# Two blocks of a network on one core: the order of the first loads, the first expert pair, the scattered pairs, and the start of the second block

## The chip, the cores and the metric

The kernel runs on one core of a Trainium2 chip. Its time is the device time of one execution in microseconds (us). Three runs of the kernel before gave 2696.38 us in the median, 2688.37 to 2698.73. All stages follow each other on that one core: TensorE (PE) with its weight loads (PEld), VectorE (DVE), ScalarE (ACT), GpSimd (POOL) and SyncE (SP), which mainly issues DMA transfers.

## The reference, cut to what matters

There are 512 tokens of 1024 channels in fp32 and a context of 256 rows. A first block is followed by a second one of two layers.

```python
# first block
m  = silu(c) @ w_mod + b_mod;  mc = silu(c_ctx) @ w_mod + b_mod      # shifts, scales, gates
hn = rmsnorm(x, g_norm1)*(1+sc1) + sh1;  cn = rmsnorm(ctx, g_norm1)*(1+csc1) + csh1
z  = hn @ w_in;  zc = cn @ w_in[:, OFF_BK:]     # the last 32 columns of w_in are the decay gates
h  = x + g1 * (concat(spatial_gating(z), gated_linear_attention(z, zc)) @ w_out)
hn2 = rmsnorm(h, g_norm2)*(1+sc2) + sh2
# router: 8 groups x 8 experts, top group, top 2 experts in it
for each chosen (token, expert):  y[token] += gate * (silu(t @ w1[e]) * (t @ w3[e])) @ w2[e]
h  = rmsnorm(h + g2*y, g_final)                 # input of the second block
# second block, layer 0: bidirectional DeltaNet and pooling mixer; layer 1: short convolution;
# each layer then a feed-forward in which each of 16 experts chooses its tokens; rmsnorm at the end
```

The 64 experts of the first block hold 3 x 64 matrices of 1024 x 512, some 403 MB.

## The kernel before

Six stages run one after the other; their rough places in the profiled execution are: mixer of the first block (mix1, 0 to 350 us), its 64 experts (moe1, 350 to 1489), mixer of layer 0 (mix2, to 1857), feed-forward (ec0, to 2165), mixer of layer 1 (mix3, to 2381), feed-forward and final norm (ec1, to the end). Each stage is a set of Python generators (tasks) which a planner, `weave`, interleaves by ranks and assumed times; a task yields an event, a count of free buffers, or a number of nanoseconds. The outcome is one fixed instruction sequence per engine. That sequence isn't always the order of the text: a POOL memset of `ch` (L2326), which the text puts late in the routing, runs at 5.77 us, and the cast of `wbg` (L448) stands on ACT ahead of the squares of `h`, which come earlier in the text. Engines run their sequence in order.

**Loads.** `pump` puts weight tiles (512 KB, or 256 KB) on SP's queue whenever the planner has a buffer for them; other transfers are issued by SP, POOL or ACT where the text has them. In `start` of mix1 SP issues `h` (x, 2 MB), `cx` (context, 1 MB), `wbg` (32 columns of w_in: 1024 pieces of 128 bytes), `w2g`, and then the 16 tiles of w_mod. POOL issues constants, and L635 writes zeros (`am`, repeated) into `yd`, a DRAM buffer of 4 MB into which the experts' outputs are later scattered. `cx` and `h` are squared on ACT, `rsqrt` makes 1/rms on DVE, `dg` is that on a diagonal, and 32 and 64 fp32 matmuls of `cx` and `h` against `dg` norm and transpose at once (`pT`). Then come the rows of the modulation (`pmr`, `pmt`, in `mod_rows`), which make A and B (L669, L670); the mixer's matmuls need these.

**Experts (`moe1`, `experts1`).** Two experts are one pair, 32 pairs in all, each with 24 weight tiles; 26 tile buffers stand ready when the stage begins, and a buffer is loaded again when PE has used it. `rank` gives each (token, expert) a slot (64 to an expert). For a pair, DVE makes the one-hot matrix P (L1252), PE takes token numbers out of it (`pid`), an indirect DMA on POOL gathers those rows of `xd` (the normed tokens, written to DRAM) into `xg` (L1240), eight transposes (`pxt`) and a scale and shift (`AB`, from `scales`) give `xT`, and PE computes `pab` (w1, w3), `phT` and `py` (w2). The first FAR = 28 pairs scatter their outputs to `yd` (L1351); after the last of them, `far` reads `yd` back in four tiles (`yg`, one buffer) and adds them to `h` (L1535). The last four pairs add theirs through matmuls against P (`pcm`, L1387), with their outputs split in two parts (`out_parts`, yh and yl). `ctx2` (the context's part of block 2) and `book` are woven among the pairs. `mods2` makes modulation rows of block 2 beside the end of mix1.

**Start of mix2.** `gfb` (g_final on all partitions) is loaded by POOL; u = h * gfb on DVE; ACT squares h and u; for each of four token tiles a chain of small DVE steps (`newton`) gives a norm `cf`, its diagonal goes to PE (`pT`); four more chains give `rf`. DVE also has the sums `macc` for the modulation of layer 0 (L2190), which wait for ada_w tiles.

## Time and profile before

| | us |
|---|---|
| three runs: median (lowest to highest) | 2696.38 (2688.37 to 2698.73) |
| the profiled execution's own time | 2696.17 |
| its span in the trace | 2694.4 |
| PE busy in it | 2362.1 (88%) |
| DVE busy | 1139.8 (42%) |
| ACT busy | 655.1 (24%) |
| POOL busy | 258.5 (10%) |
| DMA | 772.58 MB, mean 287 GB/s |

The mean granted TensorE clock was 0.951 of full speed. The page of the profile divides the span into 40 slices of about 67 us; in each it gives the busy share of each engine and of the 16 DMA engines in tenths. A busy share close to 1.0 in the DMA line means that the transfers set the pace there. The other views used are windows (busy time of each engine and the DMA share in a stretch), the timeline (instructions in order of time, with the idle time before each and what released it), and the waits (who was waited for, in total, how often, and the longest).

### The profile page before, as it was taken

Reading aid. Unit: us, or ns where it says so; the run is one execution under the profiler, and the core shown is the slowest. Engines: PE = TensorE matmul, PEld = TensorE weight load, DVE = VectorE, ACT = ScalarE, POOL = GpSimd, SP = SyncE. Lnnn points to the kernel's source line nnn. Section 1 sums busy time; section 2 is a strip of 40 time slices with the busy share of each in tenths; the row PEclk is TensorE's granted clock in tenths of the full one; section 3 lists DMA queues with packets and bytes.
Section 4 is the critical chain, followed back from the end, with each engine's and each line's share of the span. In section 5 each row is a group of like instructions: output and inputs, shape, how many; then the busy total and the mean of one; then the engine's idle time right before and its main releaser. Section 6 shows DMA issues by size and latency. Waiting matters only on the chain. (4 is left out here: it accounts for less than half of the span.)

```text
span 2694.4 us, 32948 instructions
## 1 busy us (share of the span) xinstructions
PE 2362.1 (88%) x11811; PEld 1302.3 (48%) x11811; DVE 1139.8 (42%) x2995; ACT 655.1 (24%) x1360; POOL 258.5 (10%) x257
## 2 busy tenths in 40 slices
PE   4899988899889988888869588897999989979997
PEld 3578743344333323332223467686544368854442
DVE  2878553322511111110122789696132287452223
ACT  3632432322102100111000444342211032331111
POOL 0000011001210000000000312322000010110000
PEclk9999988999999999999989799997999999989999
DMA  7545588999999999999996435535899776149984
GB/s 284 162 147 155 168 312 298 345 356 401 392 394 356 371 409 408 405 403 403 407 383 256 137 110 157 150 130 223 333 383 346 300 260 202 58 182 397 394 321 172
DMA packets 270337, 772.58 MB, mean 287 GB/s; under 512 B 42987, under 2 KB 54395, under 8 KB 269660
## 3 DMA queue, kind: packets, MB, share of 16 engines
q1 hardware_dynamic: 255964, 744.79, 74.0%
q0 software_dynamic: 12768, 23.15, 2.5%
q10 hardware_dynamic: 1440, 2.52, 0.3%
q8 instruction: 94, 1.54, 0.2%
q14 instruction: 71, 0.58, 0.1%
HBM read 767.11 MB, written 26.74 MB: 295 GB/s over the span
## 5 line engine op out<-in xcount | busy, mean ns | idle before, releaser
L1403 PE MATMUL pab<-w,xT 128*64 128x512 f32 x3072 | 814.9, 603 | 18.8 <-DMA w<-in_w_dram 18.6
L1403 PEld LDWEIGHTS pab<-w,xT 128*64 128x64 f32 x3072 | 237.4, 137 | 470.8 <-issue 353.1
L1403 PE MATMUL py<-w,hT 128*64 128x512 f32 x1536 | 378.1, 631 | 35.6 <-ACT hT L1335 32.2
L1403 PEld LDWEIGHTS py<-w,hT 128*64 128x64 f32 x1536 | 116.1, 142 | 224.8 <-issue 164.5
L386 ACT CAST wh<-w 128x512 fp32r<-128x512 f32 (+2 forms) x160 | 110.1, 695 | 227.9 <-PE pg L466 185.6
L387 DVE TENSOR_TENSOR wl<-w,wh 128x512 fp32r<-128x512 f32 (+2 forms) x160 | 134.5, 849 | 63.7 <-ACT wh L386 57.5
L1327 DVE TENSOR_TENSOR hh<-hh,pab 128x512 f32<-128x512 f32 x32 | 22.0, 687 | 328.1 <-PE pab L1403 328.0
L1387 DVE TENSOR_TENSOR h<-h,pcm 128x512 f32<-128x512 f32 x160 | 102.4, 682 | 100.4 <-PE pcm L466 100.3
L1299 ACT ACTIVATE xT<-pxt,AB 128x128 f32<-128x128 f32 x190 | 70.0, 464 | 243.0 <-PE pab L1403 224.6
L466 PE MATMUL pg<-xh,wh 128*128 128x512 f32 x288 | 118.8, 416 | 9.6 <-DVE cv L1675 9.5
L1345 DVE TENSOR_TENSOR yf<-py,g 128x512 f32<-128x512 f32 x56 | 36.2, 686 | 210.6 <-PE py L1403 210.6
L466 PE MATMUL pg<-xl,wh 128*128 128x512 f32 x288 | 115.6, 401 | 0.0
L466 PE MATMUL pg<-xh,wl 128*128 128x512 f32 x288 | 115.5, 402 | 0.0
L1325 ACT ACTIVATE hh<-pab 128x512 f32<-128x512 f32 x32 | 19.1, 597 | 371.0 <-PE pab L1403 371.0
L2190 DVE SCALAR_TENSOR_TENSOR macc<-w,c,macc 128x512 f32<-128x512 f32 x116 | 89.7, 776 | 28.7 <-DMA w<-in_ada_w_dram 15.3
L1176 DVE TENSOR_TENSOR hh<-hh,pab 128x512 f32<-128x512 f32 x16 | 11.0, 687 | 188.5 <-PE pab L1403 188.5
L472 PE MATMUL phT<-CA,hh 128*128 128x128 f32 x192 | 32.6, 294 | 63.2 <-DVE hh L1327 52.7
L1240 POOL DMA_INDIRECT xg<-xd,nt x32 | 33.0, 1030 | 525.1 <-PE pxt L472 510.3
L466 PE MATMUL pcm<-yh,PT 128*128 128x512 f32 x160 | 67.8, 437 | 9.7 <-ACT yh L1378 9.5
L1377 DVE SCALAR_TENSOR_TENSOR yo<-py,gt,g 128x512 f32<-128x512 f32 x40 | 30.0, 751 | 105.5 <-PE py L1403 103.8
L1378 ACT CAST yh<-yo 128x512 fp32r<-128x512 f32 x40 | 24.7, 618 | 203.4 <-DVE yo L1377 203.4
L466 PE MATMUL pdis<-P,xh 128*128 128x256 f32 x256 | 68.1, 303 | 4.6 <-DVE P L1107 4.6
(758 smaller groups left out, 3777.7 us busy)
## 6 DMA issues: line engine op xcount, KB each, us to landing
w<-in_w_dram SPq DMA_DIRECT2D x768, 512.0 KB, 10.2
w<-in_w_gate_dram SPq DMA_DIRECT2D x128, 512.0 KB, 9.1
w<-in_w_up_dram SPq DMA_DIRECT2D x128, 512.0 KB, 10.1
w<-in_w_down_dram SPq DMA_DIRECT2D x128, 512.0 KB, 8.2
w<-in_ada_w_dram SPq DMA_DIRECT2D x164, 256.0 KB, 3.1
w<-in_w_mod_dram SPq DMA_DIRECT2D x64, 256.0 KB, 2.9
w<-in_sc_w_in_dram SPq DMA_DIRECT2D x24, 512.0 KB, 5.3
w<-in_w_in_dram SPq DMA_DIRECT2D x40, 256.0 KB, 2.8
```

The lines of the kernel that those rows point to most:

```text
L386: nc.scalar.copy(hi, raw)
L387: nc.vector.tensor_tensor(lo, raw, hi.bitcast(F32), op=ALU.subtract)
L466: ins = self.nc.tensor.matmul(out, lhsT, rhs, start=start, stop=stop)
L472: self.nc.tensor.transpose(out, in_, self.ident if ident is None else ident)
L1240: nc.gpsimd.indirect_dma_start(out=xg[pr % len(xg)], out_offset=None, in_=xd, in_offset=bass.IndirectOffsetOnAxis(ap=d, axis=0), bounds_ch ...
L1299: nc.scalar.activation(xT[:, k0 + k, :], p[:, k * 128:(k + 1) * 128], AF.Identity, scale=self.Af[:, k0 + k:k0 + k + 1], bias=self.Bf[:, k0 ...
L1345: nc.vector.tensor_tensor(y[:, c * 512:(c + 1) * 512], ps[c], self.g2[:, c * 512:(c + 1) * 512], op=ALU.mult)
L1377: nc.vector.scalar_tensor_tensor(y, p[:rows], gate[:rows], self.g2[:rows, c * 512:(c + 1) * 512], op0=ALU.mult, op1=ALU.mult)
L1378: nc.scalar.copy(yh[:rows], y)
L1387: self.nc.vector.tensor_tensor(self.h[:, i, cs], self.h[:, i, cs], p, op=ALU.add)
L1403: self.nc.tensor.matmul(out, lhsT, rhs, start=start, stop=stop)
L2190: nc.vector.scalar_tensor_tensor(acc, w, s, acc, op0=ALU.mult, op1=ALU.add)
```

## The change

- First loads: `cx` is issued before `h`; `wbg` is issued after `pump`, behind all the weight tiles that `pump` has queued on SP by then; `w2g` goes to POOL's queue, ahead of POOL's constants.
- The zeros for `yd` stand at the end of `start` in the text, behind the splits of the modulation.
- `scales` (the pfc matmuls and the copy to AB) moves from the start of `moe1` into the routing tail of mix1; the later rows of `mods2` are held until the rank is made.
- First expert pair: no token numbers and no gather. Pr = P * r (four DVE steps) and 32 fp32 matmuls of h against Pr give the scaled, transposed tokens directly. The three gather buffers are for later pairs.
- FAR goes from 28 to 30, so two pairs are left to `pcm`; yh and yl have two buffers instead of three in this stage; the work tiles of the pairs are allocated up front.
- mix2: the row of g_final is loaded when moe1 begins; the eight `newton` chains become two vector `rsqrt`, one for cf and one for rf.

```diff
-FAR = 28
+FAR = 30
@@ first loads, mix1
+        cx = bg.tile([128, NTC, D], F32, tag="cx", name="cx")
+        nc.sync.dma_start(cx, a["ctx"].rearrange("(i p) d -> p i d", p=128))
         if self.h_in is None:
             nc.sync.dma_start(self.h, a["x"].rearrange("(i p) d -> p i d", p=128))
-        cx = bg.tile([128, NTC, D], F32, tag="cx", name="cx")
-        nc.sync.dma_start(cx, a["ctx"].rearrange("(i p) d -> p i d", p=128))
-        wg = self.t512(tp, "wbg")[:, 0:KD * 32].rearrange("p (k f) -> p k f", k=KD)
-        nc.sync.dma_start(wg, w_in[:, BG:BG + 32].rearrange("(k p) f -> p k f", p=128))
-        w2 = cp.tile([33, 512], F32, name="w2g")
-        nc.sync.dma_start(w2, a["w_gate2"])
...
         self.pump()
+        wg = self.t512(tp, "wbg")[:, 0:KD * 32].rearrange("p (k f) -> p k f", k=KD)
+        nc.sync.dma_start(wg, w_in[:, BG:BG + 32].rearrange("(k p) f -> p k f", p=128))
+        w2 = cp.tile([33, 512], F32, name="w2g")
+        nc.gpsimd.dma_start(w2, a["w_gate2"])
@@ consts() loses, start() gets at its end
+            nc.gpsimd.dma_start(self.yd.rearrange("(p r) d -> p r d", p=128),
+                                am.rearrange("p a b c t -> p (a b c t)").unsqueeze(1).to_broadcast([128, 2 * T // 128, D]))
@@ tail, after the rank; mod_rows
             self.rk = self.rank(self.Mb, NE1)
+            self.fire(evr, 0)
...
         for j in range(len(wants)):
+            if j and hold:
+                yield hold
@@ experts1: feed, and the transposes of pair 0
                 if not pr:
-                    yield rG
-                    yield 700
-                    fetch(pr, number(Pq, tok, 2 * pr, T, "nt"))
+                    Pr = work.tile([128, NT, 128], F32, tag="PT", name="Pr", bufs=3)
+                    for i in range(NT):
+                        nc.vector.tensor_scalar(Pr[:, i, :], Pq(i).bitcast(F32), self.r[:, i:i + 1], None, op0=ALU.mult)
+                    hot.append(Pr)
+                    self.fire(evn[0], 300)
...
-                    self.tr(p[:, k * 128:(k + 1) * 128], self.fcol(x, k0 + k))
+                    if pr:
+                        self.tr(p[:, k * 128:(k + 1) * 128], self.fcol(x, k0 + k))
+                        continue
+                    for i in range(NT):
+                        self.mm(p[:, k * 128:(k + 1) * 128], self.fcol(self.h[:, i], k0 + k), hot[0][:, i, :], start=(i == 0), stop=(i == NT - 1))
@@ mix2
-            for i in range(NT):
-                nc.vector.tensor_scalar(t[i][:, 0:1], s2[:, i:i + 1], 1.0 / D, r[:, i:i + 1], op0=ALU.mult, op1=ALU.add)
-                self.newton(t[i], c[:, i:i + 1])
-                nc.vector.tensor_scalar(dg3[:, i, :], self.ident, c[:, i:i + 1], None, op0=ALU.mult)
-            dg = dg3
+            nc.vector.scalar_tensor_tensor(v, s2, 1.0 / D, v, op0=ALU.mult, op1=ALU.add)
+            dg = self.diag(cp, self.rsqrt(cp, v, [128, NT], "cf"), NT, dg3)
...
-            for i in range(NT):
-                nc.vector.tensor_copy(t[i][:, 0:1], s1[:, i:i + 1])
-                self.newton(t[i], r[:, i:i + 1])
+            r = self.rsqrt(cp, s1, [128, NT], "rf")
```

## Rows read from the trace of the kernel before

**Rows 1.** Profile page: busy tenths of PE and DMA in 40 slices of the span.

```profile
PE   4899988899889988888869588897999989979997
...
DMA  7545588999999999999996435535899776149984
```

**Rows 2.** Timeline, 0 to 61 us: start, duration, engine, line, out<-in [idle before <-releaser].

```profile
0.75 0.44 SPq L570 DMA_DIRECT2D h<-in_x_dram  x1
...
4.94 0.80 POOL L635 DMA_DIRECT2D yd<-am  x1
...
18.65 1.06 ACT L205 ACTIVATE junk<-cx 128x1024 bf16<-128x1024 f32 x1 [8.73 <-DMA cx<-in_ctx_dram]
...
26.23 0.40 ACT L448 CAST wbgh<-wbg 128x256 fp32r<-128x256 f32 x1 [5.39 <-DMA wbg<-in_w_in_dram]
...
34.77 0.16 DVE L179 TENSOR_SCALAR n1v<-n1s 128x4 f32<-128x4 f32 x1
...
37.98 10.29 PE L466 MATMUL pT<-dg,h 128*128 128x128 f32 x64 [2.69 <-issue]
...
60.25 0.24 DVE L670 SCALAR_TENSOR_TENSOR A<-A,V 128x8 f32<-128x8 f32 x2
```

**Rows 3.** Windows: busy PE, PEld, DVE, ACT, POOL (instructions), PEclk, DMA share, GB/s.

```profile
45.00:50.00 5.00, 5.00 (x50) 3.68 (x52) 1.81 (x3) 1.17 (x2) 0.00 (x0) 1.00 1.04 364
50.00:55.00 5.00, 5.00 (x48) 2.11 (x40) 0.00 (x0) 1.59 (x4) 0.00 (x0) 1.00 0.02 5
80.00:100.00 20.00, 19.29 (x75) 12.42 (x76) 15.74 (x28) 16.40 (x23) 1.10 (x2) 1.00 0.73 233
```

**Rows 4.** Timeline, 366 to 383 us: the first expert pair.

```profile
366.85 0.88 DVE L1252 TENSOR_TENSOR P<-slot,CA 128x128 fp32r<-128x128 f32 x4
...
367.27 0.98 PE L466 MATMUL pid<-tk,P 128*128 128x2 f32 x4 [2.10 <-DVE P L1252]
...
369.46 1.19 POOL L1240 DMA_INDIRECT xg<-xd,nt  x1 [3.01 <-issue]
...
380.95 1.97 PE L1403 MATMUL pab<-w,xT 128*64 128x512 f32 x2
```

**Rows 5.** Windows of the experts' stage.

```profile
365.00:370.00 5.00, 1.15 (x9) 1.01 (x6) 4.58 (x22) 1.28 (x2) 1.99 (x3) 0.50 0.94 336
410.00:415.00 5.00, 5.00 (x20) 1.49 (x18) 1.22 (x5) 0.17 (x1) 0.00 (x0) 0.73 0.21 85
415.00:420.00 5.00, 4.62 (x26) 2.13 (x22) 1.16 (x2) 0.00 (x0) 0.51 (x1) 1.00 0.00 0
420.00:425.00 5.00, 5.00 (x26) 1.84 (x27) 0.60 (x4) 0.00 (x0) 4.62 (x8) 1.00 0.34 60
860.00:865.00 5.00, 5.00 (x25) 2.56 (x24) 0.69 (x1) 0.80 (x2) 0.00 (x0) 1.00 0.68 234
```

**Rows 6.** Waits of SP's queue, 410 to 430 us: total, times, longest.

```profile
SPq L318 <- PE pab L1403: 20.5, 3, 19.7
```

**Rows 7.** Waits of PE, 1340 to 1490 us.

```profile
PE phT L472 <- DVE hh L1327: 22.2, 4, 19.6
```

**Rows 8.** Timeline of DVE and POOL, 1315 to 1490 us.

```profile
1335.70 0.59 POOL L1532 DMA_DIRECT2D yg<-yd  x1 [6.21 <-DMA yd<-yf,id]
...
1367.56 1.28 DVE L1535 SCALAR_TENSOR_TENSOR h<-yg,gk,h 128x1024 f32<-128x1024 f32 x1 [8.45 <-DMA yg<-yd]
...
1470.86 0.69 DVE L1327 TENSOR_TENSOR hh<-hh,pab 128x512 f32<-128x512 f32 x1 [9.70 <-PE pab L1403]
```

**Rows 9.** Timeline, 1489 to 1511 us: start of mix2.

```profile
1489.87 0.53 POOL L2390 DMA_DIRECT2D gfb<-in_g_final_dram  x1
...
1496.53 4.63 DVE L2417 TENSOR_TENSOR u<-h,gfb 128x1024 f32<-128x1024 f32 x4 [2.62 <-DMA gfb<-in_g_final_dram]
...
1505.28 0.75 DVE L2190 SCALAR_TENSOR_TENSOR macc<-w,c,macc 128x512 f32<-128x512 f32 x1 [1.23 <-DMA w<-in_ada_w_dram]
...
1510.42 9.85 PE L466 MATMUL pT<-gfb,h 128*128 128x128 f32 x64 [23.51 <-DVE gfb L2428]
```

More of the change, by code (lines that the diff above doesn't have):

```diff
@@ L491, in run @@
         self.ke = 2
-        self.nB, self.nX, self.nE = (n * 4 // self.ke for n in (7, 6, 12))
+        self.nB, self.nX, self.nE = 14, 12, 24
         self.psum = ctx.enter_context(tc.tile_pool(name="psum", bufs=4, space=bass.MemoryType.PSUM))
@@ L518, in run @@
         self.B2 = per.tile([128, KD], F32, name="B2")
+        self.AB = per.tile([128, 2, KD], F32, name="AB")
+        self.Af, self.Bf = self.AB[:, 0], self.AB[:, 1]
         self.g2 = per.tile([128, D], F32, name="g2")
@@ L957, in route @@
             yield 3000
-            for r, g in self.tail(tp, wr, 72, evA2, evho, br, xs=lambda c: cp.tile([128, 512], F32, tag=("R", "wsp")[c], name="xs")):
+            evr = Ev()
+            for r, g in self.tail(tp, wr, 72, evA2, evho, br, evr=evr, xs=lambda c: cp.tile([128, 512], F32, tag=("R", "wsp")[c], name="xs")):
                 self.spawn(r, g)
@@ L969, in route @@
                     x.place = place
-            self.spawn(60, self.mods2(tp, t[:, (KD + 1) * 72:], m2))
+            self.spawn(60, self.mods2(tp, t[:, (KD + 1) * 72:], m2, evr))
         evA2, evho = Ev(), {(i, c): Ev() for i in range(NT) for c in range(2)}
@@ L1058, in fcol, with scales @@
         return x[:, k // 2 * 256 + k % 2:(k // 2 + 1) * 256:2]
-    def scales(self, pool):
+    def scales(self):
         nc = self.nc
@@ L1212, in experts, with experts1 @@
         return tasks
-    def experts1(self, ws, pool, work, xd, xg, tok, ids, far):
+    def experts1(self, ws, pool, work, xd, xg, ids, far):
         nc = self.nc
@@ L1227, in experts1 @@
         evk = [Ev() for _ in range(2)]
+        hot = []
+        for tag, shape, dt, n in (("yf", [128, D], F32, 2), ("hh", [128, FF], F32, 2), ("hT", [128, 4, 128], F32, 2), ("yo", [128, 512], F32, 1),
+                                  ("id", [128, 1], U32, 12)):
+            work.tile(shape, dt, tag=tag, name=tag, bufs=n)
         def number(Pq, v, e, off, tag):
@@ L1303, in spread @@
                     yield 0
-            rG.n += 1
+            if pr:
+                rG.n += 1
             self.fire(evx[pr], 2000)
@@ L1375, in out_parts @@
         y = work.tile([128, 512], F32, tag="yo", name="yo", bufs=1)[:rows]
-        yh, yl = (work.tile([128, 512], F32R, tag=n, name=n, bufs=3) for n in ("yh", "yl"))
+        yh, yl = (work.tile([128, 512], F32R, tag=n, name=n, bufs=self.ny) for n in ("yh", "yl"))
         nc.vector.scalar_tensor_tensor(y, p[:rows], gate[:rows], self.g2[:rows, c * 512:(c + 1) * 512], op0=ALU.mult, op1=ALU.mult)
@@ L1443, in moe1 @@
             self.pump()
-            self.scales(xp)
             for x in xg:
@@ L1538, in moe1 @@
             self.tb = 2
-            self.weave(self.experts1(ws, fp, fp, xd, xg, tok, (evr, rows, evf), FAR)
+            self.weave(self.experts1(ws, fp, fp, xd, xg, (evr, rows, evf), FAR)
                        + [(950, far()), (400, book()), (900, self.ctx2(900, more, wx.close, places))])
@@ L2114, in ctx2, with mods2 @@
             last()
-    def mods2(self, tp, t, wants):
-        yield from self.mod_rows(tp, t, wants, self.c2, self.mc)
+    def mods2(self, tp, t, wants, hold):
+        yield from self.mod_rows(tp, t, wants, self.c2, self.mc, hold)
     def mods2_end(self):
@@ L2134, in mods5, with mod_rows @@
         self.fire(self.evm5, 500)
-    def mod_rows(self, tp, t, wants, cT, out):
+    def mod_rows(self, tp, t, wants, cT, out, hold=None):
         nc = self.nc
@@ L2251, in out_items, with tail @@
         return [dict(it, w=w[0], cb=cb(0)), dict(it, w=w[1], cb=cb(1), free=free, big=big, order=order or range(len(w[1].ev)))]
-    def tail(self, tp, wr, n, evm, evh, br=None, rank=1.5, sp=None, xs=None):
+    def tail(self, tp, wr, n, evm, evh, br=None, rank=1.5, sp=None, xs=None, evr=None):
         nc = self.nc
@@ L2275, in prep @@
             self.fire(evw, 500)
+            yield 1000
+            self.scales()
         G = self.gates(n) if n == NE2 else self.lg
@@ L2413, in start @@
             u = bg.tile([128, NT, D], F32, tag="xn", name="u3")
-            s1, s2, r, c = (cp.tile([128, NT], F32, name=n) for n in ("s1", "s2", "rf", "cf"))
-            t = [cp.tile([128, 4], F32, name=f"nf{i}") for i in range(NT)]
+            s1, s2, v = (cp.tile([128, NT], F32, name=n) for n in ("s1", "s2", "vf"))
             for i in range(NT):
@@ L2583, in ec @@
         with ExitStack() as st:
-            self.scales(self.x_tiles(st, E))
+            self.x_tiles(st, E)
             G = self.G
```

26 lines of the change are left out of this document (11 added, 15 removed).

## The prediction

> **What bounds the kernel now.** I read the page's slices first, then windows of each stretch that the change touches, then the timeline and the waits inside them. The slices [rows 1] show no single limit. From the sixth to the twenty-first slice (the experts) the DMA digit is 8 or 9: there the weight stream sets the pace, and PE, also near 9, follows it. In the first slice DMA is busy while PE stands at 4, and before and after the experts PE is the busier of the two. So the change has to be priced place by place, each time by what ends last there.
>
> At the start DMA is saturated until 50 us (1.04 at 364 GB/s) and then empty (0.02) [rows 3]. PE waits for a chain: the context is squared on ACT at 18.65, a cast of wbg at 26.23 comes next on ACT after a wait of 5.39 for wbg's DMA, the norm of h begins on DVE at 34.77, its 64 products on PE at 37.98, and A and B are ready at 60.25 + 0.24 [rows 2]. At the entry to the experts, P begins at 366.85, the gather is issued at 369.46, and the first pab runs only from 380.95 [rows 4]. The consequence lies later: from 410 to 425 the DMA share is 0.21, 0.00 and 0.34 [rows 5], because SP's queue waited 20.5 us, 19.7 of it at once, for pab to give weight buffers back [rows 6]. That is idle time of the engine that sets the pace: 5 x (0.79 + 1.00 + 0.66) = 12.3 us. Near the end of the stage PE waits 22.2 us, 19.6 at once, for hh [rows 7], which stands on DVE behind the read-back of yd: its reads begin at 1335.70, and the third is added from 1367.56 [rows 8]. At the start of mix2 PE has been idle for 23.51 us when pT begins at 1510.42 [rows 9].
>
> **The change part by part.**
>
> *First loads.* Two conditions end the modulation. By bytes: cx 1 MB, h 2 MB, 16 tiles of w_mod 8 MB, the zeros 4 MB if they are still issued near 4.94 [rows 2], and about half a MB of constants are 16.3 million bytes; at 370 GB/s that is 44 us, from about 2 us on, so 46, and one of four rounds of rows behind it. Those four rounds and A/B took from 48.27 (end of h's products) to 60.25, 12.0 us or 3 each [rows 2]: 49. By work: if h shares the queues with the zeros, it lands behind some 6 MB, at 19; four squares at 1.06 each (the price of the context's, equally large) take 4.5 with their reads of the sum; norm to first product was 34.77 to 37.98, 3.2; products 10.3; rounds 12.0: again 49. Gain 60.25 - 49 = 11 us. wbg is no longer needed before the casts; its consumer, the decay gates, comes after the modulation. If the zeros really are issued behind the modulation, bytes give 34 + 3 and work 11 + 4.5 + 3.2 + 10.3 + 12.0 = 41; gain 19, less what 4.2 million bytes (11 us of DMA) cost later. From 80 to 100 the DMA share is 0.73 [rows 3], so some 5 of the 11 fit there, and at most 6 are paid: 13 to 19. I take 11, since POOL had no work in front of the zeros and the order on its queue need not follow the text. The lower end is the cast: while it holds ACT and DVE until wbg lands, the squares of h stand behind it as they did now for 5.39 us. Bounds -20 (worked out as a rival below) to 19. w2g on POOL costs one issue ahead of the constants, under 1 us by the zeros' issue of 0.80 [rows 2]; nothing near waits for the constants, and without that cover it would cost that 0.8.
>
> *Held rows and scales.* The rows of mods2 are wanted by block 2 only; held, they run on PE while DVE makes slot and P, where PE was busy 1.15 of 5 us [rows 5]. They might stand ahead of the first pair's products. I put 0, with up to 3 us of the next term lost. The scales are off this path either way. The wait holds its own task and what stands behind it on PE, not SP's weights.
>
> *First expert pair.* Removed are the number product (0.98), the gather (issued at 369.46), eight transposes and the wait between. Added are four DVE steps of 128x128, which by the four of P (0.88 together [rows 4]) take about 1 us, and 32 fp32 products of 128x128x128: the 64 of h took 10.29 [rows 2], so 32 take 5.2, and the first half, which lets pab begin, 2.6. P is done at 367.7, Pr at 369, half of the products at 371.6, its scale and shift at about 373: pab starts 8 us earlier. Its weights are there: the stream has filled at a share of 0.94 or more since 365 [rows 5]. The idle stretch can shrink by 12.3 at most; 8 us of earlier start is the direct part, and the product's work while PE is otherwise idle brings the rest nearer. I take 10, bounds 5 (mods2 in front) and 12.3. The stage behind it is paced by the stream, so what it gains at 411 to 424 it keeps where the DMA share is near 1. Not everywhere: in 860 to 865 PE is busy 5.00 of 5 and DMA 0.68 [rows 5]; there PE, also started earlier, has to keep the lead.
>
> The granted clock in 365 to 370 was 0.50, the 1.2 GHz level, with PE busy 1.15 of 5 us [rows 5]. The Trainium skill (TensorE: Matmul & The Clock Gate, Part 1: The HAM clock gate) says that the throttled level is the default and that activity releases it; the row agrees. By that rule products and held rows would bring the 2.4 GHz level to pab sooner, the term would be the full 12 and the time 2666; the sum here doesn't count it.
>
> *FAR = 30.* The read-back moves two pairs later, and with it the stalled hh: it now hits pair 30 of 0 to 31 rather than 28. Two pairs lose their pcm matmuls and the adds to h behind them, which overlap PE and DVE work of the next pair. After hh of the last pair (1470.86 [rows 8]) the stage's end is unchanged in kind. If the stall went away, 19.6 would come back [rows 7]; if hh stood behind one more read, it would cost another (1367.56 + 1.28 - 1335.70)/3 = 11 us [rows 8]. The reads are still serial through one buffer, so I keep the stall and take 3, nearest to the row of unchanged reads; bounds -11 and 19.6. The last two pairs with two yh/yl buffers cost nothing: each pair has two halves.
>
> *mix2.* gfb is no longer issued at 1489.87 nor waited for at 1496.53 [rows 9]. ACT can square h and u from 1489 on: eight at 1.06 and a few weight casts end near 1500.5. One rsqrt of about eleven steps took, with its diagonal, 3.2 us at the start [rows 2]: pT at about 1503.8, against 1510.42 [rows 9], gain 6.6. But DVE had two macc steps ahead of its norm, the second from 1505.28 to 1506.0, waiting for ada_w [rows 9]; left there, pT begins near 1509, gain 1.5. I take 4. The second rsqrt is off PE's path.
>
> **Sum.** 11 + 0 + 10 + 3 + 4 = 28. The profiled execution took 2696.17, 1.77 more than its span of 2694.4, and stands 0.2 under the median of the runs, so no further correction: 2696 - 28 = **2668 us**.
>
> **The rivals.**
> 1. *The zeros do move.* For it: their place in the text; against: memset ch, late in the text, ran on POOL early. Start 13 to 19, about 17: 2662.
> 2. *The cast is in the way in part*, of one engine or behind the squares: the start gives nothing: 2679. For it: it stood ahead of h's squares before. Against: wbg's issue is now behind 8 MB, so an order made by readiness would put it later.
> 3. *The experts give the lead back.* PE sets the pace in stretches such as 860 to 865, and the woven context work may make PE wait in new places: pair term 0, FAR 1: 2680. Against: PE too starts 8 us earlier.
> 4. *The cast stays ahead of all squares of h* (slower side). The place is ACT's order around 26 us, the price follows wbg's landing: in SP's order it is behind everything queued, which kept DMA saturated until 50 [rows 3]. From there squares, norm, products and rounds take 4.5 + 3.2 + 10.3 + 12.0 = 30: 80 instead of 60, loss 20. With the other terms at their middle (17) that is 2699; with their lower ends (5, 0, 1.5) it is 2709. It decides from a landing at 47, where the loss eats the 17.
> 5. That the rank, the scratch or the products don't do what the diff says I see no way for; the first rival is the only part that might not happen.
>
> **How the numbers follow.** Forecast 0.50; first rival 0.15, second 0.15, third 0.12, fourth 0.08. About 0.5% (13 us) is what a measurement of this kernel can tell from no change, so faster means under 2683. The forecast's own bounds (start 8 to 12, pair 5 to 12.3, FAR 0 to 6, mix2 1.5 to 6.6) give 2659 to 2681; the first rival with high ends reaches 2653, the second with lower ends 2688. Range 2652 to 2688, which leaves out the fourth rival and the far ends of FAR. Faster: 0.50 + 0.15, two thirds of the second and of the third: 0.80; slower by over 0.5% only part of the fourth: 0.04.
>
> **What would show it.** In the trace after: A at about 49, ACT's cast behind h's squares, the issue of yd<-am near 5 us; pab at 373 and no DMA share under 0.7 between 405 and 430; the longest wait phT <- hh still about 20 us, one or two pairs later in number; PE's idle time before mix2's pT 4 to 7 us shorter. I am wrong if the cast waits on ACT ahead of h, if SP still waits more than 10 us for pab before 430, or if the stage of the experts isn't shorter by about 10.

## The result: 26 us slower, and the profile after

The changed kernel takes 2720.41 us in the median of four runs (2713.79 to 2724.14); the kernel before, run beside it, 2694.91 (2688.37 to 2698.73). The ratio is 1.0094 with an interval of 1.0065 to 1.0124, so slower by about 25 us, where 2668 and a gain of 28 were forecast. The profiled execution is the fastest of the four, 2713.79, with a span of 2712.0: it stands 17.6 over the span of before, some 7 less than the medians differ. Where those 17.6 us arise can be followed by the same event in both timelines (us from the span's start). Single executions scatter here: the last store of xd comes at 356.16 in before, but at 354.06 and 352.10 in the kernels `plan` and `far` below, which are the same up to there, so differences under some 4 us tell little.

| event | before | after | difference |
|---|---|---|---|
| first product of h against its diagonal (pT) | 37.98 | 64.16 | +26.2 |
| A ready | 60.25 | 84.53 | +24.3 |
| last tokens of xd written (issue) | 356.16 | 377.22 | +21.1 |
| first pab | 380.95 | 390.96 | +10.0 |
| hh of pair 0 | 405.52 | 422.30 | +16.8 |
| hh of pair 27 | 1315.43 | 1335.47 | +20.0 |
| hh of pair 31 | 1470.86 | 1485.36 | +14.5 |
| pT of mix2 | 1510.42 | 1525.15 | +14.7 |
| end of the span | 2694.4 | 2712.0 | +17.6 |

So the start loses 24 us. The entry to the experts gains 11 at the first pab, of which 4 are left at hh of pair 0 and 1 at hh of pair 27; the last four pairs gain 5.5; the start of mix2 gains nothing, and 2.9 more are lost behind it.

First the slices of PE and DMA from the page of after (busy tenths; they answer [rows 1]):

```profile
PE   1999998999989998888886587896999989979997
...
DMA  8345559999999999999997434536899876249984
```

PE's digit in the first slice is 1 where it was 4. The timeline of after at the start (start, duration, engine, line, operation, idle before and its releaser; it answers [rows 2]):

```profile
4.54 0.91 POOL L686 DMA_DIRECT2D yd<-am  x1
...
9.68 1.04 ACT L205 ACTIVATE junk<-cx 128x1024 bf16<-128x1024 f32 x1
...
43.19 0.38 SPq L586 DMA_DIRECT2D wbg<-in_w_in_dram  x1
...
47.66 1.15 ACT L386 CAST wh<-w 128x256 fp32r<-128x256 f32 x3 [35.81 <-DMA w<-in_w_in_dram]
48.10 0.43 DVE L387 TENSOR_TENSOR wl<-w,wh 128x256 fp32r<-128x256 f32 x1 [35.85 <-ACT wh L386]
...
49.38 0.40 ACT L448 CAST wbgh<-wbg 128x256 fp32r<-128x256 f32 x1 [0.56 <-DMA wbg<-in_w_in_dram]
49.69 1.05 ACT L205 ACTIVATE junk<-h 128x1024 bf16<-128x1024 f32 x1
...
52.88 5.75 PE L466 MATMUL pT<-dg,cx 128*128 128x128 f32 x32 [52.88 <-DVE dg L219]
...
56.12 1.06 ACT L205 ACTIVATE junk<-h 128x1024 bf16<-128x1024 f32 x1
...
64.16 2.05 PE L466 MATMUL pT<-dg,h 128*128 128x128 f32 x8 [5.53 <-issue]
...
84.53 0.24 DVE L672 SCALAR_TENSOR_TENSOR A<-A,V 128x8 f32<-128x8 f32 x2
```

cx now lands early (its square runs at 9.68, before at 18.65), and the zeros are still issued at 4.54. But ACT stands for 35.81 us behind its next instruction, a cast of a tile of w_in (`wh<-w`, L386, a helper's line), which waits for that tile's DMA; DVE stands 35.85 us behind the tile's low part (`wl`, L387), ahead of the last steps of cx's own norm. Then comes the cast of wbg, whose DMA was issued only at 43.19, and only then, from 49.69 to 57.1, the four squares of h. PE does nothing up to 52.88. The sequence of ACT as built shows the same without any time (before, then after; it is fixed before the run):

```
before                                after
L205 ACTIVATE junk,n1cs<-cx x2        L205 ACTIVATE junk,n1cs<-cx x2
                                      L386 CAST wh<-w x3
L448 CAST wbgh<-wbg                   L448 CAST wbgh<-wbg
L205 ACTIVATE junk,n1s<-h x2          L205 ACTIVATE junk,n1s<-h x2
L212 COPY raw<-pT                     L212 COPY raw<-pT
```

So in both kernels wbg's cast stands ahead of h's squares; in after its load is late, and three more casts stand there with it. The norm of h, its products, the four rounds of rows and A follow from 57.1 to 84.5, as the fourth rival had worked them out (80).

Windows of after (busy PE, PEld, DVE, ACT and POOL with their instructions, PEclk, DMA share, GB/s; they answer [rows 3, 5]):

```profile
45.00:50.00 5.00, 0.00 (x0) 0.00 (x0) 1.31 (x6) 1.78 (x5) 0.00 (x0) 1.00 1.06 324
80.00:100.00 20.00, 15.16 (x105) 12.03 (x105) 15.64 (x42) 12.99 (x28) 1.36 (x2) 0.91 0.13 38
365.00:370.00 5.00, 5.00 (x30) 4.21 (x29) 3.59 (x19) 2.63 (x5) 0.71 (x2) 1.00 0.27 105
390.00:395.00 5.00, 4.45 (x21) 1.68 (x20) 4.05 (x26) 0.92 (x2) 0.00 (x0) 1.00 1.03 417
395.00:400.00 5.00, 3.53 (x16) 2.46 (x16) 2.59 (x13) 0.00 (x0) 1.10 (x1) 0.83 1.03 410
400.00:405.00 5.00, 4.18 (x19) 4.21 (x20) 2.17 (x10) 0.00 (x0) 2.20 (x2) 0.50 1.03 406
410.00:415.00 5.00, 5.00 (x29) 2.83 (x25) 2.53 (x9) 3.84 (x10) 1.99 (x2) 1.00 1.03 407
415.00:420.00 5.00, 5.00 (x25) 1.84 (x27) 0.88 (x4) 1.30 (x2) 0.00 (x0) 1.00 1.03 401
...
435.00:440.00 5.00, 5.00 (x27) 2.23 (x28) 3.42 (x14) 0.00 (x0) 2.33 (x4) 1.00 0.36 81
475.00:480.00 5.00, 5.00 (x19) 2.13 (x17) 1.34 (x4) 1.72 (x4) 1.70 (x3) 0.82 0.52 144
```

From 45 to 50 DMA is saturated as before, but PE has 0.00 busy where it had 5.00. From 80 to 100 the DMA share is 0.13 (before 0.73), while PE is only beginning the mixer. At 410 to 420, where before had its hole (0.21 and 0.00), the share is 1.03; but pab begins 10 us later here too, and the hole comes later and smaller, 0.36 at 435 to 440, with another of 0.52 at 475 to 480. The waits of after say who was waited for (SP's queue from 410 to 430 us, the window of [rows 6], and from 400 to 500; PE from 1340 to 1505; total, times, longest; [rows 6, 7]):

```profile
SPq L318 <- PE pab L1421: 3.4, 5, 1.7
...
SPq L318 <- PE pab L1421: 41.7, 33, 12.3
...
PE phT L472 <- DVE hh L1345: 19.5, 4, 17.0
```

Up to 430 SP hardly waits for pab any more; its long wait of 12.3 us comes between 430 and 445. PE still waits 17.0 us at once for hh. The entry and the end of the experts in the timeline of after ([rows 4, 8]):

```profile
379.89 0.11 PEld L2180 LDWEIGHTS pmr<-wkT,wr 128*32 128x32 f32 x2 [1.21 <-issue]
...
381.67 0.89 DVE L1262 TENSOR_TENSOR P<-slot,CA 128x128 fp32r<-128x128 f32 x4
...
386.39 4.01 PE L466 MATMUL pxt<-Pr,h 128*128 128x128 f32 x32
...
390.96 3.65 PE L1421 MATMUL pab<-w,xT 128*64 128x512 f32 x14 [0.55 <-ACT xT L1316]
...
401.02 1.20 PE L466 MATMUL pxt<-Pr,h 128*128 128x128 f32 x4
...
403.80 3.41 PE L466 MATMUL pxt<-Pr,h 128*128 128x128 f32 x22
...
1446.83 1.28 DVE L1550 SCALAR_TENSOR_TENSOR h<-yg,gk,h 128x1024 f32<-128x1024 f32 x1 [8.36 <-DMA yg<-yd]
1448.03 0.68 DVE L1345 TENSOR_TENSOR hh<-hh,pab 128x512 f32<-128x512 f32 x1
...
1485.36 0.69 DVE L1345 TENSOR_TENSOR hh<-hh,pab 128x512 f32<-128x512 f32 x1 [9.69 <-PE pab L1421]
```

The rows of mods2 (`pmr`) run ahead of the products (`pxt<-Pr,h`), and pab follows P by 9.3 us where it took 14.1 before. But the 32 records at 386.39 are only the first half of the products: each fp32 product leaves two records in these traces (32 products in the code, 64 records). The second half runs from 401.02 to 407.20, behind the token numbers (`pid`) of later pairs, and only then can pair 0's pab go on. The stalled hh is that of pair 30 (1448.03), behind the third of four serial reads of yd. Last the start of mix2 ([rows 9]):

```profile
1503.44 1.06 ACT L196 ACTIVATE junk<-h 128x1024 bf16<-128x1024 f32 x1 [5.05 <-DVEq L1565]
...
1515.52 0.75 DVE L2207 SCALAR_TENSOR_TENSOR macc<-w,c,macc 128x512 f32<-128x512 f32 x1 [4.62 <-POOL macc L2201]
...
1519.02 0.69 DVE L387 TENSOR_TENSOR wl<-w,wh 128x512 fp32r<-128x512 f32 x1
...
1524.81 0.88 DVE L219 TENSOR_SCALAR dg<-CA,cfy 128x128 f32<-128x128 f32 x4
...
1525.15 7.00 PE L466 MATMUL pT<-dg,h 128*128 128x128 f32 x48 [23.69 <-DMA w<-in_ev_w_in_dram]
```

The squares end near 1512.7; pT begins 21.7 us after the first square, before 21.5 (1488.89 to 1510.42). Three sums `macc`, the first after a wait of 4.62 us for POOL, and three low parts `wl` of weights stand on DVE inside the two norms.

### The profile page after: what moved, and what is told of

Read it like the earlier page. It is cut to its first block, busy times and chain, and to the rows that moved or that the text cites. A ratio compares the mean times of both kernels' runs of the same rounds, so it can differ in the third digit from the quotient of the medians.

```text
span 2712.0 us, 32850 instructions
## 1 busy us (share of the span) xinstructions
PE 2353.7 (87%) x11807; PEld 1298.0 (48%) x11807; DVE 1121.4 (41%) x2915; ACT 655.8 (24%) x1357; POOL 261.2 (10%) x259
## 5 line engine op out<-in xcount | busy, mean ns | idle before, releaser
L387 DVE TENSOR_TENSOR wl<-w,wh 128x512 fp32r<-128x512 f32 (+2 forms) x160 | 134.6, 850 | 98.7 <-ACT wh L386 94.9
L386 ACT CAST wh<-w 128x512 fp32r<-128x512 f32 (+2 forms) x160 | 109.4, 694 | 262.4 <-PE pg L466 178.2
L1405 DVE TENSOR_TENSOR h<-h,pcm 128x512 f32<-128x512 f32 x144 | 91.9, 681 | 91.4 <-PE pcm L466 91.3
L466 PE MATMUL pcm<-yh,PT 128*128 128x512 f32 x144 | 60.8, 437 | 8.7 <-ACT yh L1396 8.5
L466 PE MATMUL pdis<-P,xl 128*128 128x256 f32 x256 | 67.4, 300 | 0.0
```

The source lines that it names most:

```text
L386: nc.scalar.copy(hi, raw)
L387: nc.vector.tensor_tensor(lo, raw, hi.bitcast(F32), op=ALU.subtract)
L466: ins = self.nc.tensor.matmul(out, lhsT, rhs, start=start, stop=stop)
L1405: self.nc.vector.tensor_tensor(self.h[:, i, cs], self.h[:, i, cs], p, op=ALU.add)
```

## The experiments

Three theories went in. **Order on the engines** (S): the start's loss is the place of the w_in casts and of wbg's cast in ACT's and DVE's fixed sequences, ahead of h's squares. **The loads themselves** (L): h and cx behind each other, the zeros and bytes set the start. **Order of the experts** (O): the products are worth little, and what decides the stage is the sequence that the planner makes of pairs and context work; its rival (W): more work on PE, or the products' own place. All medians, with the ratio to the kernel before run beside each; two kernels are best compared by their ratios. The last two columns are read from the traces: how many of the experts' weight tiles SP issues ahead of the first tile of ev_w_in (the context's part of block 2), and the MB moved from 365 to 1300 us (GB/s of windows times their length; kernels that reach the stage 20 us later lose 1 to 3 MB by that).

| kernel | median us | ratio | interval | tiles ahead | MB |
|---|---|---|---|---|---|
| before | 2692 to 2695 | 1 | | 42 | 356.6 |
| after | 2720.4 | 1.0094 | 1.0065 to 1.0124 | 58 | 353.5 |
| loads | 2721.3 | 1.0100 | 1.0080 to 1.0119 | 42 | 355.9 |
| rest | 2692.5 | .9995 | .9984 to 1.0005 | 58 | 356.2 |
| wbgfirst | 2700.2 | 1.0025 | 1.0010 to 1.0039 | 58 | 356.0 |
| fix | 2692.3 | .9987 | .9977 to .9997 | 58 | 357.0 |
| fixz | 2696.8 | 1.0014 | .9997 to 1.0031 | 58 | 357.0 |
| pair | 2701.7 | 1.0029 | 1.0017 to 1.0041 | 58 | 356.4 |
| pair3 | 2688.1 | .9980 | .9970 to .9989 | 68 | 363.2 |
| pairp | 2680.4 | .9955 | .9940 to .9971 | 68 | 365.7 |
| plan | 2681.2 | .9958 | .9943 to .9972 | 66 | 363.0 |
| late4 | 2689.3 | .9984 | .9971 to .9997 | 66 | 361.5 |
| far | 2685.6 | .9977 | .9966 to .9988 | 42 | 358.3 |
| fixm | 2683.1 | .9966 | .9955 to .9978 | 58 | 358.2 |
| nopair | 2685.0 | .9973 | .9961 to .9986 | 42 | 359.1 |
| best | 2666.9 | .9907 | .9891 to .9923 | 68 | 365.5 |
| best5 | 2665.5 | .9896 | .9878 to .9913 | 92 | 366.8 |
| best_b | 2666.2 | .9908 | .9886 to .9929 | 68 | 365.7 |

### Which part loses the time: loads, rest

`loads` is the kernel before with the first loads and the place of the zeros alone; `rest` is the changed kernel with the first loads as before.

Both carry or lack these lines of the diff shown ahead of the prediction:

```diff
+        nc.sync.dma_start(cx, a["ctx"].rearrange("(i p) d -> p i d", p=128))
             nc.sync.dma_start(self.h, a["x"].rearrange("(i p) d -> p i d", p=128))
...
         self.pump()
+        wg = self.t512(tp, "wbg")[:, 0:KD * 32].rearrange("p (k f) -> p k f", k=KD)
+        nc.sync.dma_start(wg, w_in[:, BG:BG + 32].rearrange("(k p) f -> p k f", p=128))
...
+        nc.gpsimd.dma_start(w2, a["w_gate2"])
```

> The kernel before with the first loads alone changed (context ahead of h, wbg behind the queued weight tiles, w2g on POOL, zeros later in the text). Theory A, the fixed order on ACT and DVE: three casts of a w_in tile and the cast of wbg stand ahead of h's squares and wait for tiles that land behind 16 w_mod tiles, so A and B come about 24 us later (at 84 instead of 60), the first mixer ends 20 to 22 us later, and the whole is 18 to 25 us slower than before. Rival B, that the loss sits in the experts' stage or in the second block: within 5 us of before.

> The changed kernel with the first loads as they were before; all other parts of the change stay. Theory A: the other parts together give 4 to 10 us (5 at the end of the experts, 2 at their entry, about 0 at the start of mix2), so 2685 to 2691. Rival B: slower than before, since the loss is in these parts.

`loads` takes 27.9 us more than before beside it, the whole loss and a little over; `rest` is not told from before. So the other four parts together are worth about 0, not 17, and not the 4 to 10 expected here either. In the trace of `loads` A is ready at 85.06 and ACT's cast of w_in waits 35.6 us, as in after.

### The start: wbgfirst, fix, fixz

`wbgfirst` is after with wbg issued right behind h again; cx stays first.

```diff
             nc.sync.dma_start(self.h, a["x"].rearrange("(i p) d -> p i d", p=128))
+        wg = self.t512(tp, "wbg")[:, 0:KD * 32].rearrange("p (k f) -> p k f", k=KD)
+        nc.sync.dma_start(wg, w_in[:, BG:BG + 32].rearrange("(k p) f -> p k f", p=128))
...
         self.pump()
-        wg = self.t512(tp, "wbg")[:, 0:KD * 32].rearrange("p (k f) -> p k f", k=KD)
-        nc.sync.dma_start(wg, w_in[:, BG:BG + 32].rearrange("(k p) f -> p k f", p=128))
```

> The changed kernel with one transfer moved back: wbg is issued ahead of the queued weight tiles (context, h, wbg, then w_mod); everything else as changed. Theory A: with wbg early, its cast is ahead of h's squares as it was before, but the casts of the w_in tiles come after the modulation, so ACT waits only a few us; A and B at 49 to 57 us, against 84.5 with the change, and the total 22 to 32 us below the changed kernel, 2688 to 2698. Rival: the w_in casts alone hold ACT, wbg's place doesn't matter: A and B at 80 or later.

A is ready at 61.68, no better than before (60.25): wbg's cast runs at 26.32 after 14.79 us of waiting, and the squares of h behind it. That takes the loss of the start away (the time falls by some 20 us against after), so the part that lost was the late load of wbg with what the sequence put around it; cx ahead of h gains nothing while a cast stands ahead of h's squares. The expectations of an A at 49 to 57 and of a total up to 2698 were missed. It also stays 8 us above `rest`, which has the loads of before (1.0025 against .9995, the intervals apart); in the two traces A is 4.6 us later (61.68 against 57.11), the last store of xd 1.7 and the end 6.1, and why it grows behind the experts stays open.

`fix` keeps the loads of after and changes only the sequence: casts of wbg and w_in and the sums macc are queued on ACT and DVE behind the copies of h's transposed products (`late`, which stands around each of them), and wbg has another place in SBUF.

```diff
+    def late(self):
+        with ExitStack() as st:
+            for x in self.hold.values():
+                st.enter_context(self.tc.issue_after(x))
+            yield
-            self.split2(wgh, wgl, wg)
+            with self.late():
+                self.split2(wgh, wgl, wg)
...
-                    self.evac(s.raw[:, k, :], ...)
+                    x_ = self.evac(s.raw[:, k, :], ...).ins
+                    self.hold[str(x_.engine)] = x_
-        wg = self.t512(tp, "wbg")[:, 0:KD * 32]...
+        wg = cp.tile([128, 4, 128], F32, tag="R", name="wbg")[:, 0:2, :]...
```

> The changed kernel with one thing added: the casts of wbg and of the first w_in tiles, and the sums of the context's modulation, are queued on ACT and DVE behind the copies of h's transposed tiles; wbg lies in the place of a tile that is needed later, not in the ring of work tiles. Theory A: the norm of h starts when h has landed, A and B are ready at 47 to 52 us, 9 to 13 us sooner than before and some 33 sooner than with the change; the whole is 2668 to 2682. Rival C, that the loads themselves are late (h behind the zeros, the w_mod tiles by their bytes): A and B at 58 or later, no better than the first loads of before.

The timeline of fix at the start (line numbers are one to ten higher than in after):

```profile
26.28 9.06 PE L474 MATMUL pT<-dg,h 128*128 128x128 f32 x64 [5.26 <-issue]
...
51.70 0.16 DVE L682 SCALAR_TENSOR_TENSOR A<-A,V 128x8 f32<-128x8 f32 x1
...
63.84 0.40 ACT L456 CAST wbgh<-wbg 128x256 fp32r<-128x256 f32 x1
```

The products of h begin at 26.28 instead of 64.16, A is ready at 51.70, and wbg's cast comes at 63.84. The sequence was the cause: the loads are those of after to the byte. But the time is 2692.3, not 2668 to 2682. Of the 8.5 us that A gained on before, 4.4 are left at the last store of xd (351.73 against 356.16), and even these aren't told from scatter: `plan` and `far`, which start like before, have 354.06 and 352.10 there, `fixm` and `best`, which start like fix, 355.66 and 352.50. At the end the ratio is .0008, some 2 us, under that of `rest`, which has the same edits with the loads of before, and the intervals overlap. What the loads could give at all was therefore at most a few us, not the 11 of the sum. Part of the reason is visible: the casts that were held now follow the squares, and PE waits in 50 to 140 us for `wh` 3.0 and for `cvk` 2.3 us; the rest wasn't traced.

`fixz` holds the zeros too:

```diff
-            nc.gpsimd.dma_start(self.yd..., am...)
+            tc.keep_in_program_order(nc.gpsimd.dma_start(self.yd..., am...))
```

> As the run before it (casts queued behind h's copies), and the zeros are held on POOL's queue behind the last split of the modulated h, which the diff's text had meant but the queue did not do. If the 4 MB of zeros are what the w_mod tiles wait for: A and B at 40 to 46 us, 4 to 8 sooner than with the zeros early, and the whole 2 to 8 us faster than that run. Rival: the zeros then meet the weight tiles of the mixer and the gain is paid back: within 3 us of it or slower.

A is ready at 47.77, 4 us sooner again (40 to 46 was expected), but the last store of xd is 361.04, 9.3 us later than in fix, and the time 2696.8. So moving the zeros, the first rival's gain, is paid back more than once within the same stage. From 58 to 110 us ACT waits 14.2 us for tiles of w_in where it waits 3.9 in fix, and from 60 to 80 the DMA engines move 303 GB/s instead of 191. That points to the 4 MB on the queues at that time rather than to what stands on POOL behind the held issue, but no run separates the two.

### The experts: pair, pair3, pairp, nopair

`pair` is before with the scales, held rows, products, up-front work tiles and two-buffer yh and yl; loads, FAR and mix2 as before. `pair3` does each of the 32 products three times; `pairp` does them once but tells the planner three times their price.

The first hunk makes pair3, the second pairp:

```diff
-                    for i in range(NT):
+                    for i in 3 * list(range(NT)):
...
                     for i in range(NT):
+                        e0 = self.pe
                         self.mm(p[...], self.fcol(self.h[:, i], k0 + k), hot[0][:, i, :], ...)
+                        self.pe += 2 * (self.pe - e0)
```

> The kernel before with the first expert pair by products alone (with the scales in the tail, the held rows and the two-buffer yh and yl that go with it); first loads, FAR = 28 and mix2 as before. Theory G, that the experts' stage gives the lead back: pab starts 10 to 13 us sooner, the DMA gap at 411 to 424 shrinks by about 8 us, pairs up to 600 us run 8 to 11 us sooner, and from 900 us on the lead is under 2 us, because new gaps open around 670 to 720, where PE sets the pace; total within 3 us of before. Rival K, that the lead is kept (as I had predicted): hh of pair 27 is 8 to 12 us sooner and the total 2682 to 2688.

> The kernel of the run with the first pair by products, with each of its 32 products done three times (64 products more, about 8 us of PE at the entry; the result is the same). If the entry's time is what the stage's length hangs on (rival K): hh of pair 27 and the total 6 to 9 us later than with the products once. Theory G: within 2 us of it from 900 us on.

> The kernel with the first pair by products alone, its 32 products done once, but the planner counts them three times, as in the run with three times the products. It asks whether the 13 us between those two runs came from the order in which the planner puts the pairs and the context's work on PE, or from the products themselves. Theory O (order): hh of pair 27 at 1296 to 1306 and total 2683 to 2693, like the run with three times the products. Rival V (the products themselves, by the clock or by the buffers they hold up): like the run with the products once, total 2697 to 2705.

pab begins at 369.32 in `pair`, 11.6 us sooner than before, and the kernel is 8 us slower by the ratio, outside both expectations. With 64 products more (`pair3`: pab at 378.69, 9.4 later than in `pair`) it is 13 us faster than that, which neither expectation foresaw. So neither PE's added work nor pab's start is what sets the time. `pairp` has the same matmuls, VectorE and POOL steps and transfers as `pair`, only in another sequence, and takes 21.3 us less, 20 by the ratios: theory O, with even more gained than it said. The windows of before, pair and pairp (columns as above):

```profile
365.00:500.00 135.00, 112.03 (x498) 48.71 (x495) 54.30 (x216) 37.25 (x78) 21.69 (x31) 0.85 0.91 348
500.00:700.00 200.00, 183.09 (x875) 81.78 (x877) 61.89 (x187) 47.38 (x113) 21.34 (x24) 0.98 0.98 366
```

```profile
365.00:500.00 135.00, 115.96 (x548) 53.86 (x549) 47.16 (x183) 31.82 (x69) 20.69 (x29) 0.93 0.95 360
500.00:700.00 200.00, 181.39 (x852) 81.00 (x848) 64.76 (x199) 54.44 (x121) 18.64 (x20) 0.98 0.96 356
...
1100.00:1300.00 200.00, 178.27 (x746) 64.25 (x742) 22.27 (x54) 21.39 (x51) 12.05 (x12) 0.98 1.02 404
```

```profile
365.00:500.00 135.00, 120.64 (x589) 57.36 (x590) 51.36 (x200) 35.22 (x77) 20.30 (x27) 0.94 1.01 393
500.00:700.00 200.00, 186.90 (x900) 84.77 (x898) 65.50 (x203) 49.90 (x114) 21.02 (x24) 0.99 1.01 382
...
1100.00:1300.00 200.00, 176.47 (x726) 62.51 (x724) 22.05 (x52) 24.10 (x58) 10.03 (x10) 0.98 1.03 405
```

From 1100 on pair and pairp move 404 to 405 GB/s, so there the stream sets the pace; before that pair moves 360 and 356 GB/s in the first two stretches where pairp moves 393 and 382. Against before, pair gains 12 GB/s in the first stretch (1.6 MB) and gives 10 back in the second (2.0 MB): that is where its lead goes. From pair to pairp the sum to 1300 us is 9.3 MB more, and 9.3 MB at 404 GB/s are 23 us: about the difference of the times. In the table this sum follows the column beside it: kernels that issue 42 or 58 tiles ahead of the context's first move 356 to 359 MB, those with 66 to 92 move 361 to 367 (after and loads, which come to the stage late, 353 to 356).

`nopair` asks for the worth of the products at the other end: all of fixm (below), but the first pair by gather, with scales, rows and work tiles as before.

```diff
-                    Pr = work.tile([128, NT, 128], F32, tag="PT", name="Pr", bufs=3)
...
+                    yield rG
+                    yield 700
+                    fetch(pr, number(Pq, tok, 2 * pr, T, "nt"))
```

> The best version so far without the first pair's products: first loads as changed with the casts queued behind h's copies, FAR = 30, and the vector norm of mix2 with macc and wl behind it; the first pair is gathered as before and the scales and mods2 are as before. If the products with what goes along are worth nothing (alone they were 8 us slower than before): total 2674 to 2683, equal to or below the version with them (2683). If they carry part of that version's gain: 2686 to 2694.

2685.0 against 2683.1 with the products: no difference that the intervals tell, and between the two ranges expected.

### The order alone: plan, late4

`plan` is the kernel before, gather and all, with nothing but the count: 6830 ns more at each half of pair 0's transposes. `late4` is pair with the context held until pair 4 begins, and no count changed. The first hunk makes plan, the second late4:

```diff
                     self.tr(p[...], self.fcol(x, k0 + k))
+                if not pr:
+                    self.pe += 6830.0
...
-            yield self.evf[0]
+            yield self.evf[4]
             gone = self.wless("e", more)
```

> The kernel before, with nothing changed but the planner's count: at the two halves of the first pair's transposes it is told 6830 ns of TensorE time more each, as in pairp; gather, products, loads and every other instruction are those of before, only their order can differ. Theory (the order alone is worth the 21 us of pairp against pair, and needs no products): 2672 to 2684, as pairp (2680). Rival (the order pays only where the products give pab its earlier start): 2690 to 2697. Second rival (the charge moves the order either way at random): outside both, also above 2697.

> The kernel pair, with the context's part of block 2 held until pair 4 begins rather than pair 0; no count of the planner is changed. In pairp the context's products began one or two pairs later than in pair. If this later beginning is what the 21 us are, 2680 to 2690 (pair: 2702). If it is the order as a whole, later pairs too, 2698 to 2705.

`plan` takes 2681.2, with a ratio of .9958 where pairp has .9955: the same gain without any product. SP's queue in pair and in plan (timeline; x is the count of loads in a row):

```profile
380.69 55.10 SPq L318 DMA_DIRECT2D w<-in_w_dram  x33
435.88 0.38 SPq L321 DMA_DIRECT2D w<-in_ev_w_in_dram  x1
```

```profile
383.07 53.35 SPq L318 DMA_DIRECT2D w<-in_w_dram  x40
440.12 0.38 SPq L321 DMA_DIRECT2D w<-in_ev_w_in_dram  x1
```

By these rows, which begin in the middle of the stream, plan issues 40 tiles from 383.07 until the context's first tile, pair 33 from 380.69 (from the start of the stage 66 and 58). plan's DMA share from 410 to 435 is 1.03; before it was 0.52, pair's is 0.80. So the 12.3 us hole of [rows 5], which the products were to fill, vanishes by the sequence alone, with pab at 378.85 instead of 380.95. `late4` holds the context by hand and gets 66 tiles, 361.5 MB and a ratio of .9984 against pair's 1.0029: some 12 of the 20 us. The later beginning of the context is thus one cause and accounts for more than half; what remains lies in the rest of the sequence. The code says what begins there: `ctx2` takes 12 of the 26 weight buffers out of the ring (`wless`) when it starts, which leaves 14 to a pair of 24 tiles. That these buffers, rather than the context's products on PE, are what starves the stream wasn't separated.

### The read-back and mix2: far, fixm

`far` is before with the first hunk; `fixm` is fix with the second, by which the sums macc and the low parts wl of mix2 are queued on DVE behind the diagonal of its norm.

```diff
-FAR = 28
+FAR = 30
...
             dg = self.diag(cp, self.rsqrt(cp, v, [128, NT], "cf"), NT, dg3)
+            x_ = [i for i in nc.cur_bb.bb.instructions if "DVE" in str(i.engine) or "Vector" in str(i.engine)][-1]
+            self.hold = {str(x_.engine): x_}
```

> The kernel before with FAR = 30 alone. By the trace of the changed kernel: the stalled hh moves from pair 28 to pair 30 and stays at 17 to 20 us; the stage of the experts ends 4 to 6 us sooner; the total is 2687 to 2691. Rival, that nothing is gained: within 2 us of before.

> As the run with the casts queued behind h's copies, and in mix2 the sums macc and the low parts of weights (wl) are queued on DVE behind the diagonal of the norm. Theory M, that the vector norm gained nothing because macc and wl, which wait for ada_w and weight tiles, stand inside its chain on DVE: pT begins 12 to 14 us after the stage's first square instead of 21.3, and the total is 4 to 9 us below that run. Rival W: mix2 is bound further on by something else (modulation sums, gates), and the 8 us are given back inside mix2: total within 2 us of that run although pT is sooner.

`far` gains 6 us, a little more than expected; the stall is then 17.3 us long and hits pair 30. From hh of pair 27 to hh of pair 31 it takes 150.2 us, before 155.4: 5.2 of the gain are its own. In fixm's mix2 (timeline):

```profile
1482.01 1.06 ACT L197 ACTIVATE junk<-h 128x1024 bf16<-128x1024 f32 x1 [5.05 <-DVEq L1576]
...
1494.87 0.87 DVE L219 TENSOR_SCALAR dg<-CA,cfy 128x128 f32<-128x128 f32 x4
...
1495.21 5.04 PE L474 MATMUL pT<-dg,h 128*128 128x128 f32 x26 [15.19 <-DVE dg L219]
1495.66 1.89 DVE L388 TENSOR_TENSOR wl<-w,wh 128x512 fp32r<-128x512 f32 x3
```

pT begins 13.2 us after the first square, not 21.7, and the low parts come behind it. The kernel gains 6 us on fix by the ratios (9 by the medians), as theory M had it.

### Together: best, best5, best_b

`best` is fixm with pairp's count of three times, `best5` with five times, `best_b` is best once more beside best5.

> The best version so far (casts behind h's copies, products, FAR = 30, mix2's norm ahead of macc), with the planner counting the first pair's products three times. Theory O: the experts' stage ends 8 to 14 us sooner than in the version with the plain count and the total is 2669 to 2677. Rival V: no change, within 3 us of 2683.

> The kernel best, with the planner's count of the first pair's products five times rather than three times their price. If the order gets better the later the planner believes the pairs to run, at or below best (2655 to 2667); if three times was one order among several with no trend, 2667 to 2690.

> The kernel best once more, beside best5 and the other two on the same chip: 2662 to 2672, ratio to the kernel before .989 to .992. It tells what of a difference to best5 is the chip's own scatter.

best takes 2666.9 and 2666.2 in two comparisons, by the ratio 25 us less than before, and about 50 less than after, with every edit of the change in it; 2669 to 2677 was expected. best5 is the same within the intervals, though 92 tiles stand ahead of the context: beyond 68 nothing more was gained.

## Why the prediction was wrong

**First loads, +11 put down, -24 measured.** The step that failed is "wbg is no longer needed before the casts". The two conditions (bytes and work) were right as bounds and named the wrong thing as last: neither sets A, but the fixed sequence of ACT and DVE, in which casts of w_in and wbg stand ahead of h's squares. Only the cast of wbg was in my list; three casts of w_in tiles, which [rows 2] didn't show there, came with it. Worked out from 50 us, the end of the saturated DMA, the fourth rival gave A at 80 (84.5 measured) and a loss of 20; its mechanism was the right one, and its chance of 0.08 rested on the argument that an order made by readiness would put a late load's cast late. `loads` and `fix` show that this argument is false here. The range left the rival out, and so the time; even its own 2699 to 2709 counted 17 or 6.5 us from the other parts, which gave about 1. A second error lies behind it: even with the casts out of the way the 8.5 us at A left no gain at the end that can be told, while the sum counted a gain at A as a gain of the kernel.

**The zeros** stayed at 4.54, as argued; the first rival was dead, and forced (`fixz`) it would have gained nothing.

**First pair, +10 put down, about 0 kept.** The first step that failed is "8 us of earlier start is the direct part": a pab that begins sooner is not yet a pair that is done sooner. From the last store of xd to the first pab it took 13.7 us instead of 24.8, but to hh of pair 0 45.1 instead of 49.4 (48.4 in `pair`; 47.8 and 46.5 in `far` and `plan`, which gather), because the second half of the products came late. The half that lets pab begin was put at 2.6 us, since the 64 records of h in [rows 2] were read as 64 products; they are 8 x 4 products of two records each. Read so, the row gives 5.1; measured were 4.01, at a granted clock of 1.00. The rows of mods2 did stand ahead of the products. What failed next is "what it gains at 411 to 424 it keeps": in after the hole came later and smaller, with another at 475 to 480, and `pair` gives back from 500 to 700 what it gains up to 500, in another sequence of pairs and context on SP and PE. The third rival (experts give the lead back, 2680) had the outcome right but for another reason than PE's lead at 860. `plan` and `pairp` gain 11 to 12 us on before by moving more bytes from 365 to 900, no more than the hole of 12.3; but `best` lies 18 us under `nopair` (.9907 and .9973), from which it differs by the first pair, what goes with it and the planner's count, so with another sequence more was to be had than the 12.3 that were read as the most.

Of the clock, before has this row at its first pab:

```profile
380.00:385.00 5.00, 5.00 (x13) 1.50 (x11) 3.57 (x14) 1.62 (x4) 1.99 (x2) 0.50 1.03 406
```

The granted clock there was 0.50 (the 1.2 GHz level). In after it was 1.00 (2.4 GHz) at the first pab, 390 to 395, behind the held rows and the first products; then it fell to 0.83 in 395 to 400, with PE busy 3.53 of 5 us, and 0.50 in 400 to 405, where the second half of the products runs. The rule that the prediction weighed, of the Trainium skill (TensorE: Matmul & The Clock Gate, Part 1: The HAM clock gate), is that the throttled level is the default and activity releases it; the first pab of the two traces agrees. But the lower level only came later, and the 12 us that the prediction drew from the rule are not seen.

**FAR, +3 put down, 5 to 6 measured**: right in kind (stall kept, moved to pair 30, 17.0 us long in after), only the size was low.

**mix2, +4 put down, 0 measured.** The bound's lower end named it: macc steps ahead of the norm. What failed is that the middle was taken; low parts of weights, which the list hadn't, stood in the chain too. `fixm` shows that the term was there to be had, 8.5 us at pT.

**Sum.** 11 + 0 + 10 + 3 + 4 = 28 became -28 (`loads`) and +1 for all the rest together (`rest`); -25 was measured for both. The rest came to 1 us although `far` alone gives 6, which fits that `pair`, with the sequence that it brought, takes 8. Two slips in the working changed nothing: 0.50 + 0.15 and two thirds of 0.15 and 0.12 are 0.83, not 0.80, and the second rival with the lower ends comes to 2689.5, not 2688.

## What to carry to other kernels

Where a program fixes each engine's sequence, a DMA that is moved back moves every instruction that waits for it, and all that stands behind that instruction: before pricing the move, list the waiting instructions on each engine from the sequence as built, not from the text. Price a stage that the weight stream paces by the bytes that it moves in the whole stretch, not by one hole in it, and ask when buffers are taken out of its ring. A planner's assumed price is an edit of its own: try it alone before the work that it stands for.

## What the runs showed that was not expected

Work that was added made the kernel faster: 64 more fp32 products, with which the first pab began 9.4 us later, brought 13 us, and `pairp` shows that the sequence which their price produced is enough for that. And a first pab that began 11 us sooner after the last store of xd had hh of its pair only some 4 us sooner, because half of what it needs stood further back in PE's sequence.
